# A two-layer attention encoder on one core: the global branch's output projection trails its gates by four tiles in place of three

## The chip, the cores and the metric

The kernel runs on one core of one Trainium2 chip. The metric is the device time of one execution in microseconds (us), shown as the median of several runs. One execution of it was also recorded by the hardware profiler; all rows below come from that one.

## The reference

Two layers of a hybrid block run on 528 tokens (16 learned tokens, then 512 of input), each of 1024 features in float32. Cut to what matters:

```python
def hybrid_layer(x, norm_g, w_in, q_norm_g, k_norm_g, rpb, w_o_attn, w_o_na, w_out, cos, sin):
    proj = jnp.einsum('bld,de->ble', rms_norm(x, norm_g), w_in)
    qa, ka, va, za, qb, kb, vb, zb, ga, gb = split_cols(proj)
    ...                                   # per-head norm and rotary positions for qa, ka
    oa = gqa_attention(qa, ka, va) * jax.nn.silu(za)          # the global branch
    ob = neighbourhood_attention(qb, kb, vb, rpb) * jax.nn.silu(zb)
    ya = jnp.einsum('ble,ed->bld', oa, w_o_attn)
    yb = jnp.einsum('ble,ed->bld', ob, w_o_na)
    mixed = jax.nn.sigmoid(ga) * ya + jax.nn.sigmoid(gb) * yb
    return x + jnp.einsum('bld,de->ble', mixed, w_out)
```

Global attention is 8 query heads over 2 key heads, neighbourhood attention 8 heads over a window of the token grid. After the second layer a last norm follows, and the 16 learned tokens are dropped.

## The kernel before

Activations lie with the features on the partitions and the tokens along the row. Each weight tile of 128 output features comes in two halves (the input features' upper and lower four blocks). `weights` (L232) loads a half (`raw`, SyncE's queue), casts it to the upper part `whi` on ScalarE (L240) and subtracts on GpSimd to get the lower part `wlo` (L241), three halves ahead of use; the list `order` (L207 to L222) sets in what sequence. The activations are split likewise (`hh`, `hl`), and `product` (L315) makes one output tile: for each of 8 blocks of input features three matmuls, hh with whi (L325), hl with whi (L326), hh with wlo (L327). In layer 0 a tile has 528 columns, in two stretches of 264; layer 1 drops the learned tokens in its gates and keeps 512 columns in one.

After each stretch of a product, or in its middle and at its end in layer 1, `tick` is called. It advances two objects of class `Side` (L284), which hold the attention: `side_gqa` with the 16 units of global attention per layer, `side_na` with the 8 neighbourhood heads. A unit starts when its counter, modulo 4, has a set value and its inputs are there; its parts are then due so many ticks later. So the attention's matmuls lie between those of the products. A global unit makes scores (`S`), softmax, a transposition by way of DRAM, the split `pth` and `ptl` (ScalarE L193, VectorE L194), split ends `ga` (ScalarE L896, GpSimd L898), the sum `av` (L905), its upper half copied to `cmb` (ScalarE L769) and added to `oa` (L773). The fourth block of `oa` is complete after the last unit, 7_1; it is multiplied by its gate `za` (L777) and split into `oa_3a` (ScalarE) and `oa_3b` (VectorE). A neighbourhood head has scores `Sb` (read by VectorE, L990), transposed parts (`tal`, `tbl`, `na`), sums `avb` and the result `ob`. `S` and `Sb` share one PSUM tile.

The layer ends in the merge (L1144 to L1180). First the neighbourhood branch: eight gate tiles (`merge_gate`, products 34 to 41 into `mg`), and from the fourth gate on after each one the projection tile `y` of three before (`merge_half`, L1136, weights 46 to 49). Then the global branch, with gates 26 to 33 and weights 42 to 45: gate m, then y of m less 3 from the four blocks of `oa`, the add of the other branch into `ma` (L1170) and the split `mx`. `side_na.finish()` and `side_gqa.finish()`, run before the first y tile of the branch, work off what attention is left. In layer 0 an output projection (`pp` from `mx`) follows; in layer 1 the last gate's end releases `last_split`, which splits the final weights (`wl`) on ScalarE and GpSimd, and the final matmuls `pf` (L1234 to L1236) come after the last y tile.

Of the kernel before, what the change touches and what calls it, by code (L numbers as in the profile page):

```python
# [46 lines left out]
QA, KA, VA, ZA, QB, KB, VB, ZB, GA, GB = 0, 4, 5, 6, 10, 14, 18, 22, 26, 34  # L47
WOA, WOB, WOUT = 42, 46, 50
NCHUNK = 58

LAG = 3

# [41 lines left out]
def trunk_kernel(ctx: ExitStack, tc: tile.TileContext, xT, w, gn, gf, bias, rope, out):  # L96
    nc = tc.nc
# [15 lines left out]
    def slot(tag, name, dt=F32):  # L113
        n = NKEY if tag in ("KB", "KR", "K", "E") else NTOK
        t = slots.tile([P, n], dt, tag=tag, bufs=BUFS[tag], name=name)
        return t[:, :NTOK] if tag == "E" else t
# [90 lines left out]
    order = []  # L207
    for l in range(DEPTH):
        cols = [QA, QA + 1, QA + 2, QA + 3, KA, VA]
        for j in range(4):  # L210
            cols += [KB + j, QB + j, VB + j, ZB + j, ZA + j]
        order += [(l, c, i) for c in cols for i in range(2)]
        if l == 0:

            order = order[6:]
        for gate, wo in ((GB, WOB), (GA, WOA)):
            for m in range(8 + LAG):
                order += [(l, gate + m, 0), (l, gate + m, 1)] if m < 8 else []
                order += [(l, wo + (m - LAG) // 2, (m - LAG) % 2)] if m >= LAG else []
        order += [(l, WOUT + m, i) for m in range(8) for i in range(2)] if l < DEPTH - 1 else []  # L220
    place = {key: i for i, key in enumerate(order)}
    ready, loaded = [], []  # L222
# [8 lines left out]
    def weights(l, c, half, ahead=3):  # L231
        n = place[l, c, half] + ahead  # L232
        for l_, c_, i in order[len(loaded):n + 3]:
            raw = slots.tile([P, 4 * P], F32, tag="raw", bufs=BUFS["raw"], name=f"raw{l_}_{c_}_{i}")
            nc.sync.dma_start(raw, w[l_, c_][:, 4 * P * i:4 * P * (i + 1)])
            loaded.append(raw)
        for l_, c_, i in order[len(ready):n]:
            name, raw = f"{l_}_{c_}_{i}", loaded[len(ready)]
            hi, lo = (slots.tile([P, 4 * P], F32R, tag=tag, bufs=BUFS[tag], name=tag + name) for tag in ("whi", "wlo"))
            cast = nc.scalar.copy(hi, raw)  # L240
            sub = nc.gpsimd.tensor_sub(lo, raw, hi.bitcast(F32))  # L241
            split_at["weights"] = cast.ins, sub.ins
            ready.append((hi, lo))
        return ready[place[l, c, half]]
# [22 lines left out]
    def last_split(us):  # L267
        for u in us:
            hi, lo = (((key_half if tag == "KB" else lambda name, dt: slot(tag, name, dt))(f"wl{u}{tag}", F32R))[:, :4 * P]
                      for tag in ("h", KEEP[u]))  # L270
            cast = nc.scalar.copy(hi, last_raw[u])
            sub = nc.gpsimd.tensor_sub(lo, last_raw[u], hi.bitcast(F32))
            split_at["weights"] = cast.ins, sub.ins
            last_w[u] = hi, lo

    l = 0
# [39 lines left out]
    def product(l, c, rhs, full, halves=(0, 1), name="pp", spans=None):  # L316

        ws = [weights(l, c, i) for i in halves]
        n = 4 * len(ws)
        for a, b in spans or (((0, HALF), (HALF, NTOK)) if full else ((0, NREAL),)):  # L320
            ps = bank(ps_p, f"{name}{l}_{c}_{a}", "pp")[:, :b - a]
            for i in range(n):
                wh, wl = (t[:, P * (i % 4):P * (i % 4 + 1)] for t in ws[i // 4])
                rh, rl = rhs[i]
                nc.tensor.matmul(ps, wh, rh[:, a:b], start=i == 0, stop=False)  # L325
                nc.tensor.matmul(ps, wh, rl[:, a:b], start=False, stop=False)  # L326
                nc.tensor.matmul(ps, wl, rh[:, a:b], start=False, stop=i == n - 1)  # L327
                if not full and i == 3 and n == 8:
                    tick()
            with tc.high_priority():  # L330
                yield ps, a, b
            tick()
# [121 lines left out]
    for l in range(DEPTH):  # L454
        last = l == DEPTH - 1
# [371 lines left out]
        zgate, oa, o_t, newest, sums_a = {}, [None] * 4, {}, {}, {}  # L827
# [300 lines left out]
        def merge_gate(c, m):  # L1128
            t = slot("E", f"mg{l}_{c}_{m}")
            for ps, a, b in project(c + m):  # L1130
                nc.vector.tensor_mul(t[:, a:b], ps, rbc[:, a:b])  # L1131
                split_at["gate"] = nc.scalar.activation(t[:, a:b], t[:, a:b], AF.Tanh, scale=0.5)  # L1132
            return t

        def merge_half(m, t, c, br, out, spans=None):
            for ps, a, b in product(l, c + m // 2, br, full, (m % 2,), f"y{m % 2}", spans):  # L1136
                nc.vector.scalar_tensor_tensor(out[:, a:b], t[:, a:b], 1.0, ps, op0=ALU.add, op1=ALU.mult)  # L1137
                yield a, b

        mb, gates = [], {}  # L1140
        for m in range(8 + LAG):
            if m < 8:
                gates[m] = merge_gate(GB, m)
            if m == LAG - 1:  # L1144
                side_na.finish()
                while ending:
                    ending.pop(0)()
            if m >= LAG:
                mb.append(slot("B", f"mb{l}_{m - LAG}"))
                for _ in merge_half(m - LAG, gates[m - LAG], WOB, ob, mb[m - LAG]):  # L1150
                    pass
        mixed = []
        for m in range(8 + LAG):
            if m < 8:
                gates[m] = merge_gate(GA, m)
            if last and m == 7:

                weights(l, WOA + 3, 1, 1)
                with tc.issue_after(split_at["gate"].ins):
                    last_split((0, 1, 2))  # L1160
            if m == LAG - 1:
                side_gqa.finish()
            if m >= LAG:
                ma = slot("G", f"ma{l}_{m - LAG}")
                hi, lo = two("M", f"mx{l}_{m}", F32R)
                end = m == 7 + LAG
                for a, b in merge_half(m - LAG, gates[m - LAG], WOA, oa, ma):
                    if (end and full) or b == N:
                        a = a if end else 0
                        nc.vector.tensor_add(ma[:, a:b], ma[:, a:b], mb[m - LAG][:, a:b])  # L1170
                        with ExitStack() as held:
                            if last and m in (7, 8):
                                held.enter_context(tc.issue_after(split_at["weights"][0]))
                            split(hi[:, a:b], lo[:, a:b], ma[:, a:b])
                mixed.append((hi, lo))
                if last and m in (7, 8):
                    with tc.issue_after(split_at["hi"].ins):
                        last_split(((3, 4, 5), (6, 7))[m - 7])
            if last and m == 4:
                last_load(range(KT))  # L1180

# [40 lines left out]
    for f in range(2):  # L1222
        for t in range(4):
            x = xs[f, t]
            end = f == 1 and t == 3
# [89 lines left out]
```

## Time and profile before

| | us |
|---|---|
| runs | 846.31, 846.28, 844.58; median 846.28 |
| profiled execution | 845.68, of which the span from first to last instruction is 844.0 and 1.68 lie around it |
| granted TensorE clock, mean | 0.996 of full |
| TensorE (PE) busy | 821.0, 97% of the span |
| VectorE (DVE), ScalarE (ACT), GpSimd (POOL) busy | 522.8, 474.8, 422.8 |

Matmuls are pipelined: a matmul's own duration is longer than the distance to the next one's start, and it is this distance that counts for the time. "Idle before <- releaser" says how long an engine stood still before an instruction, and what ended that.

### The profile page before, as it was taken

The numbers are of one execution on the slowest core, as the hardware profiler recorded it, in microseconds if no ns is written. First come the engines' busy times: TensorE is split into PE (matmuls) and PEld (weight loads), VectorE is DVE, ScalarE is ACT, GpSimd is POOL, SyncE is SP. The second block draws the span as 40 slices with busy tenths as digits, with TensorE's granted clock in tenths as the row PEclk, the third lists the DMA queues.
The fourth block names the chain that finished last, engine by engine and source line by source line (L and its number), as shares of the span: only waits on it lengthen the run. The fifth ranks groups of instructions, "written<-read, shape, count | busy, mean of one in ns | idle before, by whom it ended". The sixth has DMA issues, their size and how long they took to land.

```text
span 844.0 us, 16154 instructions
## 1 busy us (share of the span) xinstructions
PE 821.0 (97%) x5662; PEld 757.9 (90%) x5662; DVE 522.8 (62%) x1152; ACT 474.8 (56%) x1137; POOL 422.8 (50%) x362
## 2 busy tenths in 40 slices
PE   9999999999999999899999999999999999999997
PEld 9999999999999999899998989898988787778786
DVE  7976667676765562436547656766776556545633
ACT  8654766667864563333445456675768545543422
POOL 1664545444444453654764644444545436464851
PEclk9999999999999999999999999999999999999999
DMA  7277564667454664335555585647566566444502
GB/s 277 89 195 223 133 196 116 197 195 197 147 161 118 188 178 128 108 93 150 151 141 121 152 212 154 196 160 225 153 187 197 167 193 187 140 147 140 185 3 101
DMA packets 113249, 135.00 MB, mean 160 GB/s; under 512 B 31888, under 2 KB 66192, under 8 KB 113168
## 3 DMA queue, kind: packets, MB, share of 16 engines
q1 hardware_dynamic: 112448, 132.90, 54.0%
q8 instruction: 45, 0.74, 0.4%
q10 hardware_dynamic: 720, 1.06, 0.3%
q14 instruction: 36, 0.29, 0.1%
HBM read 98.50 MB, written 21.84 MB: 143 GB/s over the span
## 4 chain that ended last, share of the span: by engine, by line
PE 85%; DVE 6%; ACT 3%; issue 2%; DMA 2%; SPq 1%; POOL 0%; POOLq 0%; DVEq 0%; ACTq 0%
PE pp L327 18%; PE pp L325 18%; PE pp L326 18%; PE av L905 4%; PE y L326 3%; PE y L327 3%; PE y L325 3%; DVE ptl L194 2%; PE avb L1052 2%; PE S L556 2%; PE S L557 2%; PE pf L1234 2%; PE pf L1236 2%; PE pf L1235 2%; PE tb L129 1%
## 5 line engine op out<-in xcount | busy, mean ns | idle before, releaser
L241 POOL TENSOR_TENSOR wlo<-raw,whi 128x512 fp32r<-128x512 f32 x210 | 287.5, 1376 | 322.2 <-ACT whi L240 262.1
L327 PE MATMUL pp<-hh,wlo 128*128 128x264 f32 (+3 forms) x1040 | 325.8, 313 | 0.6 <-POOL wlo L241 0.6
L325 PE MATMUL pp<-hh,whi 128*128 128x264 f32 (+3 forms) x1040 | 326.1, 314 | 0.3 <-DVE ma L1137 0.3
L326 PE MATMUL pp<-hl,whi 128*128 128x264 f32 (+3 forms) x1040 | 324.0, 312 | 0.0
L327 PEld LDWEIGHTS pp<-hh,wlo 128*128 128x128 f32 x1040 | 196.4, 189 | 11.2 <-POOL wlo L241 0.8
L326 PEld LDWEIGHTS pp<-hl,whi 128*128 128x128 f32 x1040 | 196.8, 189 | 9.5
L325 PEld LDWEIGHTS pp<-hh,whi 128*128 128x128 f32 x1040 | 196.2, 189 | 9.5 <-DVE ma L1137 0.5
L240 ACT CAST whi<-raw 128x512 fp32r<-128x512 f32 x210 | 128.7, 618 | 116.5 <-PE pp L326 41.4
L867 DVE STREAM_TRANSPOSE P<-P 128x512 f32<-128x512 f32 x64 | 46.4, 726 | 38.9 <-ACT P L841 38.6
L898 POOL TENSOR_TENSOR ga<-pm,ga 32x128 fp32r<-32x128 f32 x64 | 40.4, 632 | 47.9 <-issue 26.8
L194 DVE TENSOR_TENSOR ptl<-P,pth 128x512 fp32r<-128x512 f32 x64 | 55.6, 881 | 12.8 <-ACT pth L193 10.3
L1131 DVE TENSOR_TENSOR mg<-pp,rbc 128x264 f32<-128x264 f32 (+1 forms) x48 | 24.7, 515 | 50.2 <-PE pp L327 49.5
L837 DVE CUSTOM_DVE_ANT_1 P<-S,r 128x528 f32<-128x528 f32 x64 | 44.8, 700 | 14.5 <-PE S L557 13.7
L841 ACT ACTIVATE P<-P,st 128x528 f32<-128x528 f32 x64 | 47.1, 737 | 1.7
L1132 ACT ACTIVATE mg<-mg 128x264 f32<-128x264 f32 (+1 forms) x48 | 23.7, 493 | 36.9 <-DVE mg L1131 36.8
L193 ACT CAST pth<-P 128x512 fp32r<-128x512 f32 x64 | 39.2, 612 | 1.4 <-DMA P<-turn 1.3
L905 PE MATMUL av<-ptl,VA 128*128 128x256 f32 x128 | 35.0, 299 | 4.1 <-DVE ptl L194 3.7
L992 ACT ACTIVATE bias<-bias,stb 128x208 f32<-128x208 f32 (+1 forms) x64 | 31.0, 486 | 13.3 <-DVE stb L990 13.2
L326 PE MATMUL pp<-mx,whi 128*128 128x264 f32 x128 | 36.6, 286 | 0.0
L327 PE MATMUL pp<-mx,wlo 128*128 128x264 f32 x128 | 36.4, 284 | 0.0
L325 PE MATMUL pp<-mx,whi 128*128 128x264 f32 x128 | 36.3, 284 | 0.0
L840 ACT ACTIVATE st<-st 128x1 f32<-128x1 f32 x64 | 13.0, 202 | 40.9 <-DVE st L837 40.5
(534 smaller groups left out, 1727.4 us busy)
## 6 DMA issues: line engine op xcount, KB each, us to landing
raw<-in_w_dram SPq DMA_DIRECT2D x210, 256.0 KB
turn<-P SPq DMA_DIRECT2D x32, 528.0 KB
P<-turn SPq DMA_DIRECT2D x128, 128.0 KB
bias<-in_bias_dram SPq DMA_DIRECT2D x16, 480.0 KB
KB<-KB SPq DMA_DIRECT2D x24, 272.0 KB
rawl<-in_w_dram SPq DMA_DIRECT2D x16, 256.0 KB
x<-in_xT_dram SPq DMA_DIRECT2D x8, 264.0 KB
xr<-in_xT_dram SPq DMA_DIRECT2D x8, 264.0 KB
```

The source lines that it names most:

```text
L193: split_at["hi"] = nc.scalar.copy(hi, src)
L194: split_at["any"] = nc.vector.tensor_sub(lo, src, hi.bitcast(F32))
L240: cast = nc.scalar.copy(hi, raw)
L241: sub = nc.gpsimd.tensor_sub(lo, raw, hi.bitcast(F32))
L325: nc.tensor.matmul(ps, wh, rh[:, a:b], start=i == 0, stop=False)
L326: nc.tensor.matmul(ps, wh, rl[:, a:b], start=False, stop=False)
L327: nc.tensor.matmul(ps, wl, rh[:, a:b], start=False, stop=i == n - 1)
L837: newest["max"] = nc.vector.tensor_tensor_reduce(p[:n].rearrange("p (i k) -> p i k", i=2), S[:n, :, :HALF], scale[:n].unsqueeze(2).to_broa ...
L841: nc.scalar.activation(p[:n], p[:n], AF.Exp, bias=st[:n, 1:2], scale=1.0, accum_out=st[:n, 2:3] if total is None else total)
L867: nc.vector.transpose(c["both"][:n, a:b], c["both"][:n, a:b])
L898: nc.gpsimd.tensor_sub(tm[64 + 32 * t:96 + 32 * t, n * t:n * (t + 1)], m, tm[:32, :n].bitcast(F32))
L905: nc.tensor.matmul(c["av"], rows2(c["t"][i][0]), c["t"][i][1], start=i == 0, stop=i == 8)
```

## The change

A second constant, LAG_A = 4, takes the place of LAG in the global branch of both layers: y of tile m less 4 follows gate m; the list of weight halves has the same order; `side_gqa.finish()` runs one gate later. Neighbourhood branch and arithmetic are unchanged. Line numbers after it are larger by 2.

```diff
+LAG_A = 4
...
-        for gate, wo in ((GB, WOB), (GA, WOA)):
-            for m in range(8 + LAG):
+        for gate, wo, lag in ((GB, WOB, LAG), (GA, WOA, LAG_A)):
+            for m in range(8 + lag):
                 order += [(l, gate + m, 0), (l, gate + m, 1)] if m < 8 else []
-                order += [(l, wo + (m - LAG) // 2, (m - LAG) % 2)] if m >= LAG else []
+                order += [(l, wo + (m - lag) // 2, (m - lag) % 2)] if m >= lag else []
...
-        for m in range(8 + LAG):
+        for m in range(8 + LAG_A):
             if m < 8:
                 gates[m] = merge_gate(GA, m)
-            if last and m == 7:
+            if last and m == LAG_A + 4:
                 weights(l, WOA + 3, 1, 1)
                 with tc.issue_after(split_at["gate"].ins):
                     last_split((0, 1, 2))
-            if m == LAG - 1:
+            if m == LAG_A - 1:
                 side_gqa.finish()
-            if m >= LAG:
+            if m >= LAG_A:
...
```

All other lines of the diff put `m - LAG_A` where `m - LAG` stood.

**TensorE, layer 0, where the last global unit's sum `av_7_1` meets the merge.** The first y tile is `y_42` and pp_30 is the gate after gate 29. Before:

```order
L905 MATMUL av_7_1_5081<-ga_120,VA_775 128x256
L325 MATMUL y_42_0_5175<-oa_3a,whi_42_0_5103 128x264
L325 MATMUL y_42_264_5189<-oa_3a,whi_42_0_5103 128x264
L326 MATMUL y_42_0_5175<-oa_3b,whi_42_0_5103 128x264
L327 MATMUL y_42_0_5175<-oa_3a,wlo_42_0_5104 128x264
L326 MATMUL y_42_264_5189<-oa_3b,whi_42_0_5103 128x264
L327 MATMUL y_42_264_5189<-oa_3a,wlo_42_0_5104 128x264
L325 MATMUL pp_30_0_5219<-hh_0_143,whi_30_0_5109 128x264
```

And after:

```order
L907 MATMUL av_7_1_5121<-ga_120,VA_775 128x256
L327 MATMUL pp_30_0_5180<-hh_4_190,whi_30_1_5090 128x264
L328 MATMUL pp_30_0_5180<-hl_4_191,whi_30_1_5090 128x264
L327 MATMUL pp_30_264_5207<-hh_4_190,whi_30_1_5090 128x264
L328 MATMUL pp_30_264_5207<-hl_4_191,whi_30_1_5090 128x264
L329 MATMUL pp_30_0_5180<-hh_4_190,wlo_30_1_5091 128x264
L327 MATMUL pp_30_0_5180<-hh_5_203,whi_30_1_5090 128x264
```

Behind `av_7_1` there stood the six matmuls on `oa_3a` and `oa_3b`; now the second half of pp_30 stands there, 24 matmuls that use whi_30_1 and wlo_30_1, and y_42 comes behind them. Ahead of `av_7_1`, 24 matmuls of pp_30's first half took the place of 18 of y_42; its first `av` matmul now has 19 of them ahead and five behind it.

**ScalarE, same place: the casts around the copy `cmb` of `av_7_1`.** Before:

```order
L193 CAST pth_7_1_2_5045<-P_7_1_4801 128x8x2x32
L896 CAST ga_120<-pm_7_1_4969 32x128
L769 COPY cmb_5092<-av_7_1_5081 64x256
L240 CAST whi_30_0_5109<-raw_30_0_5002 128x512
L240 CAST whi_30_1_5171<-raw_30_1_5008 128x512
L193 CAST oa_3a<-oa_3_3913 128x528
```

And after:

```order
L195 CAST pth_7_1_2_5045<-P_7_1_4801 128x8x2x32
L898 CAST ga_120<-pm_7_1_4969 32x128
L771 COPY cmb_5132<-av_7_1_5121 64x256
L242 CAST whi_30_1_5090<-raw_30_1_5002 128x512
L242 CAST whi_42_0_5170<-raw_42_0_5008 128x512
L195 CAST oa_3a<-oa_3_3913 128x528
```

The cast of whi_30_0 has moved up, to where that of whi_42_0 was; whi_30_1, which the matmuls right behind `av_7_1` now use, is cast behind the copy `cmb` that reads `av_7_1`. On GpSimd wlo_30_1 likewise stands behind the unit's `ga` and the gate product `za`.

**TensorE, layer 1, scores of a neighbourhood head (`Sb`) and of a global unit (`S`).** Before, behind the last `Sb` matmul of head 0:

```order
L557 MATMUL Sb_0_7128<-KB_00_6907,QB_0a 128x208
L325 MATMUL pp_6_0_7115<-hh_4_6121,whi_6_1_7037 128x512
L326 MATMUL pp_6_0_7115<-hl_4_6122,whi_6_1_7037 128x512
...
L325 MATMUL pp_6_0_7115<-hh_7_6342,whi_6_1_7037 128x512
L326 MATMUL pp_6_0_7115<-hl_7_6343,whi_6_1_7037 128x512
L327 MATMUL pp_6_0_7115<-hh_7_6342,wlo_6_1_7038 128x512
L728 MATMUL vtb_0_7166<-ident,vb_0_6950 128x128 x3
```

And after:

```order
L559 MATMUL Sb_0_7147<-KB_00_6907,QB_0a 128x208
L327 MATMUL pp_6_0_7134<-hh_4_6121,whi_6_1_7061 128x512
L328 MATMUL pp_6_0_7134<-hl_4_6122,whi_6_1_7061 128x512
...
L327 MATMUL pp_6_0_7134<-hh_6_6269,whi_6_1_7061 128x512
L328 MATMUL pp_6_0_7134<-hl_6_6270,whi_6_1_7061 128x512
L558 MATMUL S_0_1_1_7178<-KA1h_6925,Q_0_6533 128x264
L559 MATMUL S_0_1_1_7178<-KA1l_6926,Q_0_6533 128x264
```

Eight product matmuls now lie between the end of `Sb` and a global score that uses the same PSUM tile. All 16 units of layer 1 start three ticks (one and a half products) earlier, since `finish()` in layer 0 leaves the counter of `side_gqa` one lower; the neighbourhood heads stay where they were.

## Rows read from the trace of the kernel before

**Rows 1.** The page: the chain of work that ended last, share of the span by engine.

```profile
PE 85%; DVE 6%; ACT 3%; issue 2%; DMA 2%; SPq 1%; POOL 0%; POOLq 0%; DVEq 0%; ACTq 0%
```

**Rows 2.** The view of waits of TensorE (PE), whole span: what it waited for: us in total, times, longest us.

```profile
PE av L905 <- DVE ptl L194: 3.7, 7, 0.8
PE y L325 <- ACT oa_3a L193: 2.4, 1, 2.4
PE y L325 <- ACT ob L193: 1.5, 1, 1.5
PE y L326 <- DVE oa_3b L194: 1.1, 2, 0.6
PE avb L1052 <- DVE na L798: 0.9, 1, 0.9
```

**Rows 3.** TensorE's order in time around `av_7_1` in layer 0: start us, us, engine, line, operation, count [idle before <- releaser]. 46 matmuls start from the first row up to the last, the last row not counted.

```profile
334.89 0.28 PE L325 MATMUL y<-oa_0a,whi 128*128 128x264 f32 x1
...
337.08 0.28 PE L905 MATMUL av<-pth,VA 128*128 128x256 f32 x1
...
338.59 0.28 PE L905 MATMUL av<-ga,VA 128*128 128x256 f32 x1
341.26 0.51 PE L325 MATMUL y<-oa_3a,whi 128*128 128x264 f32 x2 [2.39 <-ACT oa_3a L193]
342.29 0.39 PE L326 MATMUL y<-oa_3b,whi 128*128 128x264 f32 x1 [0.52 <-DVE oa_3b L194]
...
343.32 0.59 PE L325 MATMUL pp<-hh,whi 128*128 128x264 f32 x1 [0.28 <-DVE ma L1137]
...
346.34 0.29 PE L326 MATMUL pp<-hl,whi 128*128 128x264 f32 x1
```

**Rows 4.** Windows of the span: stretch, its us, busy us (and instructions) of PE, weight loads, DVE, ACT, POOL, then the granted clock, DMA share and GB/s.

```profile
342.00:344.00 2.00, 1.43 (x7) 1.22 (x8) 1.37 (x4) 0.62 (x1) 2.00 (x2) 0.73 0.44 131
344.00:346.00 2.00, 2.00 (x11) 2.00 (x11) 1.30 (x2) 0.63 (x1) 2.00 (x2) 0.50 0.56 157
360.00:380.00 20.00, 20.00 (x166) 20.00 (x165) 7.40 (x14) 7.07 (x14) 9.91 (x8) 1.00 0.32 92
660.00:680.00 20.00, 18.50 (x93) 15.42 (x92) 11.85 (x21) 10.51 (x25) 9.67 (x9) 1.00 0.64 206
```

**Rows 5.** ScalarE, VectorE and GpSimd in order of time, same place as rows 3.

```profile
338.90 0.36 ACT L769 COPY cmb<-av 64x256 f32<-64x256 f32 x1 [1.38 <-PE av L905]
339.29 1.14 ACT L240 CAST whi<-raw 128x512 fp32r<-128x512 f32 x2
...
336.52 1.55 DVE L194 TENSOR_TENSOR ptl<-P,pth 128x512 fp32r<-128x512 f32 x2 [1.00 <-ACT pth L193]
...
339.99 6.33 POOL L241 TENSOR_TENSOR wlo<-raw,whi 128x512 fp32r<-128x512 f32 x4 [0.25 <-ACT whi L240]
```

**Rows 6.** ScalarE, GpSimd and VectorE in order of time in layer 1, where the last neighbourhood head meets its merge.

```profile
666.49 0.37 ACT L769 COPY cmb<-av 64x256 f32<-64x256 f32 x1 [3.77 <-PE av L905]
667.28 0.62 ACT L193 CAST ob<-ob 128x512 fp32r<-128x512 f32 x1
...
662.01 1.67 POOL L898 TENSOR_TENSOR ga<-pm,ga 32x128 fp32r<-32x128 f32 x2 [1.63 <-issue]
...
665.08 0.69 DVE L777 TENSOR_TENSOR ob<-ob,zb 128x512 f32<-128x512 f32 x1 [1.72 <-POOL zb L822]
```

**Rows 7.** TensorE in order of time in layer 1, where the last global unit meets the merge.

```profile
754.53 0.40 PE L327 MATMUL pp<-hh,wlo 128*128 128x512 f32 x1
...
755.81 0.50 PE L326 MATMUL y<-oa_3b,whi 128*128 128x512 f32 x1 [0.55 <-DVE oa_3b L194]
...
756.53 0.50 PE L325 MATMUL y<-oa_0a,whi 128*128 128x512 f32 x1
```

**Rows 8.** TensorE, then VectorE, in order of time: scores of one neighbourhood head in layer 1 and their reading. Eight `Sb` matmuls begin with the first row.

```profile
501.74 0.26 PE L556 MATMUL Sb<-KB,QB_0a 128*128 128x208 f32 x1
...
502.56 0.27 PE L557 MATMUL Sb<-KB,QB_0a 128*128 128x208 f32 x1
...
502.87 0.37 DVE L990 CUSTOM_DVE_ANT_0 bias<-Sb,bias 128x208 f32<-128x208 f32 x1 [0.99 <-PE Sb L557]
...
504.19 0.08 DVE L990 DVE_READ_ACCUMULATOR2_ANT stb<- 128x1 f32 x1
```

**Rows 9.** VectorE, then TensorE, in order of time: the keys of layer 1's global attention, and the place on TensorE behind which its first scores now stand.

```profile
485.49 1.79 DVE L547 TENSOR_TENSOR KA1l<-k,KA1h 64x544 fp32r<-64x544 f32 x2 [0.71 <-ACT KA1h L546]
...
486.49 0.27 PE L728 MATMUL vtam<-ident,va 128*64 128x128 f32 x1
```

**Rows 10.** The end of layer 1: TensorE (12 matmuls of one y tile from the first row to the second), then VectorE in order of time; the last row is VectorE in layer 0.

```profile
784.13 0.40 PE L327 MATMUL y<-oa_3a,wlo 128*128 128x512 f32 x1
...
786.90 0.40 PE L327 MATMUL y<-oa_3a,wlo 128*128 128x512 f32 x1
...
791.86 0.68 DVE L1137 SCALAR_TENSOR_TENSOR ma<-mg,y 128x512 f32<-128x512 f32 x1
792.57 1.07 DVE L1170 TENSOR_TENSOR ma<-ma,mb 128x512 f32<-128x512 f32 x1
...
795.27 0.67 DVE L1137 SCALAR_TENSOR_TENSOR ma<-mg,y 128x512 f32<-128x512 f32 x1
...
380.62 0.71 DVE L1170 TENSOR_TENSOR ma<-ma,mb 128x528 f32<-128x528 f32 x1
```

More of the change, by code (lines that the diff above doesn't have):

```diff
@@ L1160, in trunk_kernel @@
                     last_split((0, 1, 2))
-            if m == LAG - 1:
+            if m == LAG_A - 1:
                 side_gqa.finish()
-            if m >= LAG:
-                ma = slot("G", f"ma{l}_{m - LAG}")
+            if m >= LAG_A:
+                ma = slot("G", f"ma{l}_{m - LAG_A}")
                 hi, lo = two("M", f"mx{l}_{m}", F32R)
-                end = m == 7 + LAG
-                for a, b in merge_half(m - LAG, gates[m - LAG], WOA, oa, ma):
+                end = m == 7 + LAG_A
+                for a, b in merge_half(m - LAG_A, gates[m - LAG_A], WOA, oa, ma):
                     if (end and full) or b == N:
                         a = a if end else 0
-                        nc.vector.tensor_add(ma[:, a:b], ma[:, a:b], mb[m - LAG][:, a:b])
+                        nc.vector.tensor_add(ma[:, a:b], ma[:, a:b], mb[m - LAG_A][:, a:b])
                         with ExitStack() as held:
-                            if last and m in (7, 8):
+                            if last and m - LAG_A in (4, 5):
                                 held.enter_context(tc.issue_after(split_at["weights"][0]))
@@ L1175, in trunk_kernel @@
                 mixed.append((hi, lo))
-                if last and m in (7, 8):
+                if last and m - LAG_A in (4, 5):
                     with tc.issue_after(split_at["hi"].ins):
-                        last_split(((3, 4, 5), (6, 7))[m - 7])
+                        last_split(((3, 4, 5), (6, 7))[m - LAG_A - 4])
             if last and m == 4:
```

## The prediction

> **What bounds the kernel now.** I read first the page's chain, then TensorE's waits, then the order in time around the largest of them. The chain lies on TensorE for 85% [rows 1], and the engine is busy for 97% of the span, so only two things can pay: TensorE's idle times, and stretches where its clock is low. The view of waits names few [rows 2]: 2.4 us before the first matmul on oa_3a, 1.1 us in two waits on oa_3b, 1.5 us on the last block ob of the neighbourhood branch, and 4.6 us in small waits inside the attention (ptl, na). The change touches the first four.
>
> The order in time shows what the one in layer 0 costs. From the first y matmul at 334.89 to 346.34, 46 matmuls start [rows 3]. At the undisturbed pace of 20 us for 166 matmuls, 0.1205 us each [rows 4], they need 5.54 us; they took 11.45. So **5.9 us are lost there**, more than the waits say: 4.5 us in the waits and the slow starts around them, and 1.45 us in the clock. After the waits the granted clock stood at 0.50, the 1.2 GHz level, for all of 344 to 346 [rows 4], and the 13 matmuls from 343.32 to 346.34 took 3.02 us for 1.57 [rows 3].
>
> **The change, part by part.**
>
> *The join in layer 0, −3.5 us.* Behind `av_7_1` the order puts pp_30's second half in place of the matmuls on oa_3. With 19 matmuls ahead in place of 18, av begins at about 337.18 in place of 337.08; its fifth pair still waits for ptl, which ends at 338.07 [rows 5], and its last matmul starts about 0.16 later than before, at 338.75. The copy `cmb` came 0.31 after the last av, and the next cast 0.39 after `cmb` [rows 3, 5]: that cast is now whi_30_1, from 339.45 to 340.05 (half of the 1.14 that two took, and the write). TensorE has nothing else ahead of it in its queue: a **new wait** of 1.2 us, from 338.87 to 340.05. Four matmuls follow (0.5). The fifth needs wlo_30_1. GpSimd began 0.70 after the cast's start [rows 5], now 340.15, and took 1.58 for one of four, so 341.73: a second wait of 1.2. Then 20 matmuls (2.4 us) run to 344.1, and under them oa_3a is cast (about 340.7 to 341.4) and oa_3b subtracted; y_42 finds both ready. The loss of 5.9 becomes 2.4. Ends: no new wait, −5.9; and the clock falls as before, −2.05. I take −3.5, since both new waits are worked out from the rows of the very instructions.
>
> *The same join in layer 1, −1.1 us.* There four distances between matmuls took 2.00 us, from 754.53 to 756.53 [rows 7]; at 0.231 each (12 in 2.77, [rows 10]) they need 0.92. With a whole gate product behind av_7_1, 24 times 0.231 or 5.5 us, both casts are done, and whi_30_1 stands where no copy holds it up for long. Ends: −1.1 and 0.
>
> *The neighbourhood join in layer 1, −1.5 us.* TensorE waits 1.5 us for ob [rows 2]. ob was late since zb stood on GpSimd behind the 1.67 us of ga of unit 4_1, VectorE waited 1.72 for zb, and the cast of ob stood behind `cmb` of the same unit, which waited 3.77 for av_4_1 [rows 6]. By the order unit 4_1 is now past that point when the last head ends: its ga comes before the head's sums, av_4_1 has one matmul left, and 12 product, 4 score and 9 y matmuls (about 5.4 us) lie ahead of the first use of ob. Ends: −1.5 and 0.
>
> *The shared score tile, +1.0 us.* As the global units of layer 1 start three ticks earlier, the second score of a unit comes in the same tick as a head's `Sb`, with eight matmuls (or 14 of the short form) between, and may not write before VectorE has read `Sb`. In the trace of before, reading ends at 504.27, 1.71 after the start of the last `Sb` matmul [rows 8]; eight matmuls later is 502.67 + 8 x 0.231 = 504.52. So 0.2 us to spare, if VectorE is free. It is busy 62% of the time; with what is left of one operation of 0.70 spread evenly, a head waits 0.62 x (0.5 x 0.5 / 2 / 0.7) = 0.11 us, eight heads 0.9. No wait on this tile is in the rows of before, so the bounds are wide: −2.3, if half of the 4.6 us of small waits [rows 2] go in the new phase, and +5, if each head meets a split pair like the 1.55 of ptl [rows 5] at its middle, 0.78 less 0.2. I stay near the row in which VectorE was ready.
>
> *First scores of layer 1, +0.3 us.* They now stand right behind vtam, 486.49, and need KA1l, which VectorE finishes at 487.28 [rows 9]; one score and two product matmuls lie between. Ends: 0 and +0.5.
>
> *The end, +0.6 us.* Behind the last gate come five y tiles in place of four. A tile takes TensorE 2.77 us, but VectorE, ScalarE and VectorE again (ma, add, mx) take 3.41 from tile to tile [rows 10]. One tile more in that chain ends the last mx later by 0.64 against TensorE, which already has almost no slack there. The final matmuls can't hide it, their last ones being the ones that use it. Ends: 0 and +1.0. One row speaks for the lower end: the add took 1.07 beside GpSimd's splits of the final weights and 0.71 alone [rows 10], and those splits, released by the last gate, begin one tile earlier as seen from the end. The Trainium skill (SBUF — State Buffer, section Who interferes with whom) states that a VectorE instruction with two SBUF inputs contends with a GpSimd instruction that reads SBUF; the trace agrees, 1.07 against 0.71. By that rule, with the splits out of the way, the tile would take 3.05 and the term be +0.3; I keep 0.6, since the splits still last through most of the tiles.
>
> *Loads, at nothing.* The sequence of weight loads has the same length, and the moved halves stay three ahead of use; no matmul waited for a load in the view of waits. If that cover went, it would show as a cast waiting for its raw.
>
> **The sum:** −3.5 − 1.1 − 1.5 + 1.0 + 0.3 + 0.6 = −4.2, against the profiled execution's 845.68: **841.5 us**. That execution lies 0.6 below the median of the runs, 846.28. About 0.2%, 1.7 us, can be told from no change.
>
> **The rivals.**
>
> *The clock falls all the same.* Two waits of 1.2 us with four matmuls between may be as bad as one of 2.4 with a few behind it. For it: in the trace of before the clock fell after 2.39, 0.52 and 0.28 us of idleness with six matmuls among them [rows 3, 4], 3.2 us in all against 2.4 now. Against it: the single wait of 1.5 us for ob left the clock at 1.00 [rows 2, 4]. It gives back 1.45: 843.0. The Trainium skill (TensorE: Matmul & The Clock Gate, section A second HAM failure mode: psum-queue depth-cycling) states that frequent short idle times between groups of matmuls, and not only one long one, can make the clock swing between its levels. By that rule this rival is the forecast; no row of before shows short waits alone doing it.
>
> *The wait only changes its name.* whi_30_1 and wlo_30_1 come later than worked out (GpSimd still at za, the cast behind something I took for done), TensorE stands as long as before in layer 0, and the layer 1 joins lose what the score tile costs. Then −1.1 − 1.5 + 1.0 + 0.3 + 0.6 = −0.7: 845.0. For it: the same chain av, cmb, cast stands there. Against it: it is shorter by the add, the gate product and oa_3b.
>
> *Slower: the score tile becomes the bound of layer 1.* Each of its eight heads would hold the global score that follows; VectorE's queue has softmax, transposition and split pairs of the neighbouring unit in just that tick. With w us per head the sum is −5.2 + 8w; it passes +1.7 from w = 0.86, and with a whole split pair ahead, w = 1.35, it gives +5.6: 851.3. For it: only 0.2 us to spare [rows 8]. Against it: VectorE began to read 0.31 us after the last `Sb` matmul in the row of before, and it idles a third of the time.
>
> **How the numbers follow.** Forecast 0.57; clock rival 0.20; name rival 0.14; slower rival 0.09. The forecast's own range, with half the bounds of its terms, is 839 to 844; it and the clock rival lie below 844.0, but for the upper edge. The range reaches to the name rival: **838.8 to 845.0**; what is left out is the slower rival and the far ends of the terms. Faster by over 0.2%: 0.74 (0.77 of the first two less their upper edges); within 0.2%: 0.17; slower: 0.09.
>
> **What would show it.** In the profile after: no wait of TensorE on oa_3a or oa_3b, and none on ob; two waits near 339 to 342, on whi (ScalarE) and wlo (GpSimd), of about 1.2 us each; granted clock at 1.00 in that stretch; waits on VectorE's reading of `Sb` before global scores in layer 1, about 1 us in all; one of some 0.3 on KA1l; and some 1 us of waits on mx among the final matmuls, 0.6 more than now. The prediction is wrong if the clock falls to 0.50 behind those two waits, if the wait on whi is over 2 us, or if layer 1 shows waits of the score tile of over 4 us.

## The result, and the profile after

The changed kernel took **841.01 us** (median of 5 runs, 837.82 to 842.12) against 845.47 (5 runs, 844.58 to 846.31): ratio **0.9942**, interval 0.9919 to 0.9965. The profiled execution took 842.12, of which 840.4 is the span, 3.6 less than the span of before. It was the slowest of its five, so the two traces show less than the medians do.

The view of waits of TensorE in the kernel after (columns as in [rows 2]):

```profile
PE av L907 <- DVE ptl L196: 2.4, 4, 1.0
PE S L558 <- DVE stb L992: 2.3, 2, 1.9
PE pp L329 <- POOL wlo L243: 2.1, 3, 1.0
PE pp L327 <- ACT whi L242: 1.1, 1, 1.1
PE S L559 <- DVE KA1l L549: 0.2, 1, 0.2
```

The waits on oa_3a, oa_3b, ob and na are gone. In their place stand waits on whi and wlo, and on VectorE's reading of the score tile (stb). No wait on mx is in the view. TensorE where `av_7_1` meets the merge in layer 0, the counterpart of [rows 3]:

```profile
338.19 0.28 PE L907 MATMUL av<-ga,VA 128*128 128x256 f32 x1
339.56 0.39 PE L327 MATMUL pp<-hh,whi 128*128 128x264 f32 x1 [1.09 <-ACT whi L242]
...
341.33 0.59 PE L329 MATMUL pp<-hh,wlo 128*128 128x264 f32 x1 [1.01 <-POOL wlo L243]
341.71 0.42 PE L327 MATMUL pp<-hh,whi 128*128 128x264 f32 x1
...
344.57 0.38 PE L327 MATMUL pp<-hh,whi 128*128 128x264 f32 x1
```

The first two waits are those forecast: 1.09 on whi_30_1 behind the last `av` matmul, four matmuls, 1.01 on wlo_30_1. But behind the second wait the distance between two starts is 0.22 in place of 0.12, until 344.57. The windows say why, the counterpart of [rows 4]:

```profile
340.00:342.00 2.00, 0.99 (x6) 0.77 (x5) 1.14 (x2) 1.70 (x4) 2.00 (x2) 0.84 0.01 4
342.00:344.00 2.00, 2.00 (x11) 2.00 (x11) 0.07 (x1) 0.00 (x0) 2.00 (x2) 0.50 0.46 132
```

The granted clock stood at 0.50, the 1.2 GHz level, from 342 to 344, so in this execution the clock fell behind the two short waits, as it had before behind the longer ones on oa_3a and oa_3b. ScalarE, then GpSimd, at the same place [rows 5]:

```profile
338.50 0.36 ACT L771 COPY cmb<-av 64x256 f32<-64x256 f32 x1 [1.55 <-PE av L907]
338.89 1.14 ACT L242 CAST whi<-raw 128x512 fp32r<-128x512 f32 x2
...
337.90 1.28 POOL L824 TENSOR_TENSOR za<-za,sumsa 128x512 f32<-128x512 f32 x1
339.59 5.88 POOL L243 TENSOR_TENSOR wlo<-raw,whi 128x512 fp32r<-128x512 f32 x4 [0.41 <-ACT whi L242]
```

The casts of whi_30_1 and whi_42_0 start 0.39 after `cmb`, and GpSimd, free since 339.18, begins wlo_30_1 0.70 after the cast's start, both as worked out.

Where the last neighbourhood head meets the merge of layer 1 (GpSimd, ScalarE, TensorE; [rows 6]), zb no longer stands behind ga, and TensorE takes the last block of ob without a wait, 2.08 after its first y matmul at 665.49:

```profile
663.34 1.30 POOL L824 TENSOR_TENSOR zb<-zb,sumsb 128x512 f32<-128x512 f32 x1
...
665.54 0.62 ACT L195 CAST ob<-ob 128x512 fp32r<-128x512 f32 x1
...
665.49 0.40 PE L327 MATMUL y<-ob,whi 128*128 128x512 f32 x1
...
667.57 0.40 PE L327 MATMUL y<-ob,whi 128*128 128x512 f32 x1
```

The longest new wait of layer 1 is on the shared score tile. SyncE's queue, then VectorE, then TensorE:

```profile
641.65 0.33 SPq L872 DMA_DIRECT2D turn<-P  x1
...
643.37 0.44 SPq L976 DMA_DIRECT2D bias<-in_bias_dram  x1
...
651.64 0.37 DVE L992 CUSTOM_DVE_ANT_0 bias<-Sb,bias 128x208 f32<-128x208 f32 x1 [2.52 <-DMA bias<-in_bias_dram]
...
653.09 0.39 PE L558 MATMUL S<-KA1h,Q 128*128 128x264 f32 x1 [1.91 <-DVE stb L992]
```

VectorE was free for 2.52 us before it read `Sb` of head 7; it waited for that head's bias, 480 KB, which SyncE issued at 643.37, behind a transfer (`turn` of unit 4_1, which carries the unit's scores to DRAM) that its queue did not issue before 641.65. The second score of unit 5_0 waited 1.91 us for the tile. In the trace of before the same load stood ahead of that `turn`, which came at 648.85:

```profile
641.02 0.41 SPq L974 DMA_DIRECT2D bias<-in_bias_dram  x1
```

The other wait on the score tile is of another kind. VectorE, then TensorE:

```profile
566.20 0.36 DVE L992 CUSTOM_DVE_ANT_0 bias<-Sb,bias 128x208 f32<-128x208 f32 x1
...
567.65 0.39 PE L558 MATMUL S<-KA1h,Q 128*128 128x264 f32 x1 [0.41 <-DVE stb L992]
```

Here VectorE came to `Sb` straight from other work, with no idle time ahead, 0.96 us after the start of the last `Sb` matmul (565.24).

The end, VectorE then TensorE [rows 10]:

```profile
781.91 0.67 DVE L1139 SCALAR_TENSOR_TENSOR ma<-mg,y 128x512 f32<-128x512 f32 x1
...
784.38 0.69 DVE L196 TENSOR_TENSOR mx<-ma,mx 128x512 fp32r<-128x512 f32 x1 [0.69 <-ACT mx L195]
784.99 0.68 DVE L1139 SCALAR_TENSOR_TENSOR ma<-mg,y 128x512 f32<-128x512 f32 x1
...
788.42 0.68 DVE L1139 SCALAR_TENSOR_TENSOR ma<-mg,y 128x512 f32<-128x512 f32 x1
...
788.67 0.39 PE L329 MATMUL y<-oa_3a,wlo 128*128 128x512 f32 x1
789.15 0.50 PE L1236 MATMUL pf<-wl0h,mx 128*128 128x512 f32 x1
```

VectorE takes 3.08 and 3.43 from tile to tile, and the first final matmul starts 0.48 after the last y matmul where 0.23 is the pace. In the experiment with the larger lag in layer 1 alone the trace names the releaser of that matmul: VectorE's ma, not mx.

Cut into stretches by the starts of four TensorE instructions (the scores' transposition tb near 241, the first output projection matmul of layer 0, vtam in layer 1, the first pf matmul; last column: to the start of the last matmul), the traces compare as follows, in us. In the line of before, tb starts at 241.18, the projection at 388.76, vtam at 486.49, pf at 792.68, the last matmul at 837.72; the other lines are read in the same way. "Again" is the changed kernel's second profile; the rest are the experiments below. "New phase" is the earlier start of layer 1's global units, which the change brings along with the lag.

| kernel | tb to projection (layer 0's join) | to vtam | vtam to pf (layer 1) | pf to last |
|---|---|---|---|---|
| before | 147.58 | 97.73 | 306.19 | 45.04 |
| after | 145.85 | 97.73 | 304.96 | 45.18 |
| after, again | 145.89 | 97.79 | 303.04 | 45.18 |
| larger lag in layer 0 alone | 144.18 | 97.80 | 306.11 | 45.00 |
| larger lag in layer 1 alone | 148.56 | 97.73 | 305.94 | 45.13 |
| new phase alone | 148.81 | 97.79 | 302.77 | 45.06 |
| whi_30_1 early | 143.50 | 97.73 | 305.34 | 45.16 |
| whi_30_1 early, lags 4 and 3 | 143.30 | 97.73 | 301.71 | 45.07 |

The untouched stretch in the middle agrees within 0.07 in all of them. That is not so everywhere: ahead of tb, where no instruction was moved either, the start of tb lies between 239.66 and 241.18 in the thirteen profiles of this document, and the old join of layer 0 took 147.58, 148.56 and 148.81. So a difference between two profiles counts here only where a wait or the clock in the rows accounts for it. Ahead of tb after stands 0.57 earlier than before: that part of the 3.6 is not the change's.

### The profile page after: what moved, and what is told of

Its sections match the earlier page's. It is cut to its first block, busy times and chain, and to the rows that moved or that the text cites. A ratio compares the mean times of both kernels' runs of the same rounds, so it can differ in the third digit from the quotient of the medians.

```text
span 840.4 us, 16156 instructions
## 1 busy us (share of the span) xinstructions
PE 821.2 (98%) x5662; PEld 758.9 (90%) x5662; DVE 521.4 (62%) x1152; ACT 474.4 (56%) x1137; POOL 424.4 (50%) x362
## 4 chain that ended last, share of the span: by engine, by line
PE 79%; DVE 7%; DMA 5%; ACT 4%; issue 2%; SPq 1%; POOL 1%; POOLq 0%; DVEq 0%; ACTq 0%
PE pp L329 17%; PE pp L328 17%; PE pp L327 17%; PE av L907 4%; PE y L329 3%; PE y L328 3%; PE y L327 3%; PE S L558 2%; PE S L559 2%; PE avb L1054 2%; PE pf L1236 2%; PE pf L1238 2%; PE pf L1237 2%; DMA bias<-in_bias_dram 1%; DVE ptl L196 1%
## 5 line engine op out<-in xcount | busy, mean ns | idle before, releaser
L900 POOL TENSOR_TENSOR ga<-pm,ga 32x128 fp32r<-32x128 f32 x64 | 42.2, 660 | 61.6 <-issue 32.6
L907 PE MATMUL av<-pth,VA 128*128 128x256 f32 x128 | 34.6, 291 | 0.0
```

The lines of the kernel that those rows point to most:

```text
L900: nc.gpsimd.tensor_sub(tm[64 + 32 * t:96 + 32 * t, n * t:n * (t + 1)], m, tm[:32, :n].bitcast(F32))
L907: nc.tensor.matmul(c["av"], rows2(c["t"][i][0]), c["t"][i][1], start=i == 0, stop=i == 8)
```

## The experiments

**The larger lag in layer 0 alone.** LAGS is a lag for each layer; the added tick restores the phase that layer 1 had.

```diff
-LAG_A = 4
+LAGS = (4, 3)
...
             if m == LAG_A - 1:
                 side_gqa.finish()
+                if not last:
+                    side_gqa.now += 1
```

> The larger lag in layer 0 alone: layer 1 keeps a lag of three, and the counter of the global units is set so that layer 1 has the phase of before. Theory (the parts add up, each worth what the two traces show at its place): the three waits on oa_3a, oa_3b and ma give way to two on whi_30_1 and wlo_30_1 of about 1.1 and 1.0 us, the clock still falls to 0.50 behind them, -1.7 us, so 843.8 against 845.5; layer 1 shows the waits of before (ob 1.5, oa_3b 0.55, no wait on the score tile). Rival (the clock fell by chance in the one execution that was profiled): the clock stays at 1.00 behind the two waits, -3.5 or so, 842.

Measured 841.25 (840.80 to 843.32), ratio 0.9962 (0.9949 to 0.9974): −3.2 us. TensorE, and windows:

```profile
338.73 0.39 PE L327 MATMUL pp<-hh,whi 128*128 128x264 f32 x1 [1.10 <-ACT whi L242]
...
340.48 0.39 PE L329 MATMUL pp<-hh,wlo 128*128 128x264 f32 x1 [1.00 <-POOL wlo L243]
...
340.00:342.00 2.00, 1.52 (x12) 1.52 (x13) 0.99 (x1) 1.01 (x2) 2.00 (x2) 1.00 0.24 71
342.00:344.00 2.00, 2.00 (x18) 2.00 (x18) 0.86 (x2) 1.27 (x3) 2.00 (x3) 1.00 0.52 184
```

The two waits are there, 1.10 and 1.00, and the clock stayed at 1.00: the rival's case. The join costs 144.18 in place of 147.58, −3.4, the forecast's −3.5. Layer 1 shows the waits of before. The profiled execution was the shortest of the five: it and two others (841.22, 841.25) show a mean granted clock of 0.999, the two longer ones (842.56, 843.32) 0.997. So the clock may well have fallen in two of the five; where, no row of theirs shows.

**The larger lag in layer 1 alone**: LAGS = (3, 4), without the added tick.

> The larger lag in layer 1 alone, layer 0 and the phase of layer 1 as before. Theory: only the wait on oa_3b in layer 1 goes (-1.1 with the slow start around it), and the end gains at most 0.6 us in waits on mx: between -1.1 and -0.5, 844.4 to 845.0; ob still waits 1.5. Rival (the join in layer 1 was hidden, since the layer's end is bound by VectorE's chain of 3.4 us a tile): no change, 845.5, with the 1.1 us back as waits on mx among the last matmuls.

Measured 844.34, ratio 0.9995 (0.9986 to 1.0004): no change. TensorE in the join of layer 1, and at the end:

```profile
755.66 0.50 PE L327 MATMUL y<-oa_3a,whi 128*128 128x512 f32 x1 [0.21 <-ACT oa_3a L195]
...
792.10 0.50 PE L1236 MATMUL pf<-wl0h,mx 128*128 128x512 f32 x1 [0.16 <-DVE ma L1139]
```

In the old phase the wait on oa_3 stays, 0.21, with slow starts around it: the stretch vtam to pf gains 0.25, and the end loses 0.09. So neither theory nor rival quite: the lag alone doesn't clear that join. The order says why: between the last `av` matmul and the first on oa_3a stand 11 matmuls before, 15 here, 20 with the new phase alone, and 44 with both.

**The new phase alone**: a lag of three in both layers.

```diff
             if m == LAG - 1:
                 side_gqa.finish()
+                if not last:
+                    side_gqa.now -= 1
```

> The earlier start of layer 1's global units alone: a lag of three in both layers, the counter of the global units one lower when layer 1 begins. Theory: the wait on ob (1.5) and one on na (0.9) go, waits of the shared score tile come (2.3 us in two), one on KA1l (0.2) and one on wlo (0.6): within 1 us of before, 844.5 to 846. The larger wait on the score tile stands where VectorE waits for head 7's bias, whose load is queued on SyncE behind the transfer turn of unit 4_1. Rival (the new phase is what carries the gain, and the wait for the bias in the profiled execution was an accident): -2.5 or more, 843 or less, and no wait of the score tile over 0.5 us in this profile.

Measured 842.34 (841.51 to 843.12), ratio 0.9968 (0.9957 to 0.9980): −2.7 us. Layer 1 gains 3.42 (306.19 to 302.77): the theory of "within 1 us" fell, the rival holds. VectorE at head 7, and TensorE's only wait on the score tile:

```profile
652.57 0.38 DVE L990 CUSTOM_DVE_ANT_0 bias<-Sb,bias 128x208 f32<-128x208 f32 x1 [0.45 <-DMA bias<-in_bias_dram]
...
570.51 0.39 PE L556 MATMUL S<-KA1h,Q 128*128 128x264 f32 x1 [0.42 <-DVE stb L990]
```

VectorE waited 0.45 for the bias here, and TensorE did not wait for that head's tile. The join with oa_3 in layer 1 shows no wait either, with a lag of three.

**The changed kernel once more.**

> The changed kernel itself once more, for the spread between its executions (837.8 to 842.1 so far). Theory: the same waits at the same places as in its first profile, with the clock falling behind whi_30_1 and wlo_30_1 and a wait of 1.9 us for head 7's bias, about 841. Rival (waits that hang on when a transfer lands come and go): the wait for the bias, or the fall of the clock, is missing in this profile, and the time is 838 to 839 in such an execution.

Measured 839.05 (837.12 to 839.86), ratio 0.9925 (0.9913 to 0.9938). Its profile, windows and VectorE at head 7:

```profile
342.00:344.00 2.00, 2.00 (x11) 2.00 (x11) 0.43 (x1) 0.29 (x1) 2.00 (x3) 0.50 0.51 181
...
649.04 0.38 DVE L992 CUSTOM_DVE_ANT_0 bias<-Sb,bias 128x208 f32<-128x208 f32 x1 [0.37 <-DMA bias<-in_bias_dram]
```

The clock fell again, and the wait of 1.91 us is missing: issue to reading took 6.1 us (642.92 to 649.04) where it had taken 8.3 (643.37 to 651.64). The rival holds in one half: the wait for the bias comes and goes, and layer 1 differs by 1.92 between the two profiles (304.96 and 303.04).

**whi_30_1 ahead of `cmb`** in the changed kernel:

```diff
+            if not last and m == LAG_A - 1:
+                weights(l, GA + LAG_A, 1, 1)
+                split_at["early"] = split_at["weights"]
             if m < 8:
                 gates[m] = merge_gate(GA, m)
...
+            with ExitStack() as held:
+                if full and "early" in split_at:
+                    held.enter_context(tc.issue_after(split_at["early"][0]))
+                nc.scalar.copy(t[r, :n], av[q, :n])
```

> The changed kernel, with whi_30_1 of layer 0 cast ahead of the copy cmb of av_7_1 on ScalarE; nothing else in the order differs. Theory (the two waits are ScalarE's and GpSimd's queues): the wait on whi_30_1 goes, and the one on wlo_30_1, still behind ga and za on GpSimd, starts earlier and grows from 1.0 to about 1.7 us (za's end to wlo's end, 1.3, and what is left of za). The loss falls from 2.1 to 1.7 us: 0.4 faster than the changed kernel, 838.6 to 840.6, less if the clock stays at 1.00 behind one wait. Rival (whi comes late for its raw data, not for its place in the queue): the wait stays on whi at about 1.1 us.

Measured 837.09 (836.06 to 839.74), ratio 0.9909 (0.9896 to 0.9922). TensorE, and windows:

```profile
340.00 0.39 PE L329 MATMUL pp<-hh,wlo 128*128 128x264 f32 x1 [1.51 <-POOL wlo L243]
...
650.44 0.39 PE L558 MATMUL S<-KA1h,Q 128*128 128x264 f32 x1 [1.89 <-DVE stb L995]
...
340.00:342.00 2.00, 2.00 (x16) 2.00 (x17) 0.99 (x3) 1.17 (x3) 2.00 (x2) 1.00 0.38 128
652.00:654.00 2.00, 2.00 (x10) 1.90 (x10) 1.68 (x4) 1.64 (x4) 0.00 (x0) 0.50 0.01 2
```

One wait of 1.51 on wlo_30_1 is left (forecast 1.7), the clock stays at 1.00 behind it, and the join takes 143.50, 2.4 less than after. The wait for the bias, 1.89, was in this profile, and here the clock fell to 0.50 behind that single wait, which it had not in after (1.00 from 652 to 656, behind 1.91). This execution took 839.74, the four others 836.06 to 837.17.

**wlo_30_1 ahead of the gate product za as well**: the product of the last unit comes one tick later, and with `issue_after` behind the early subtraction.

> The same, and on GpSimd wlo_30_1 ahead of the gate product za. Theory: one wait of about 0.4 us on wlo_30_1 is left (ga's end plus 1.3, against the end of the four matmuls on whi_30_1), the loss falls by 1.7 us, and with so little idle time the clock stays at 1.00, which gives back up to 1.5 us more in executions in which it fell: 836 to 838.5. Rival (za, now later, holds up the last block of oa): a wait on oa_3a of over 0.5 us among the matmuls of y_42, and no gain over the changed kernel.

Measured 838.47 (836.36 to 839.18), ratio 0.9918: not faster than whi_30_1 alone. TensorE, then VectorE:

```profile
338.90 0.39 PE L329 MATMUL pp<-hh,wlo 128*128 128x264 f32 x1 [0.29 <-POOL wlo L243]
...
342.51 0.36 PE L327 MATMUL y<-oa_0a,whi 128*128 128x264 f32 x1 [0.88 <-DVE mg L1143]
...
340.13 1.77 DVE L782 TENSOR_TENSOR oa<-oa,za 128x528 f32<-128x528 f32 x1 [1.15 <-POOL za L830]
341.94 0.43 DVE L1143 TENSOR_TENSOR mg<-pp,rbc 128x264 f32<-128x264 f32 x1
```

The wait on wlo_30_1 is down to 0.29, but za is late: VectorE's product with it starts at 340.13 and takes 1.77 us, the gate's instruction mg queued behind it frees its PSUM bank late, and TensorE waits 0.88 there. The join takes 143.37, 0.13 less. The rival holds in substance, with mg in place of oa_3a.

**Each head's bias in layer 1 one tick earlier**: a step of head hd at tick 3 loads the bias of hd + 1.

> The changed kernel, with the bias of each neighbourhood head of layer 1 loaded one tick earlier, so that head 7's load stands ahead of unit 4_1's transfer turn on SyncE. Theory (the long wait on the score tile is that load, queued behind a transfer that waits for VectorE): no wait of VectorE on bias, none of TensorE on the score tile over 0.5 us, in any execution; the slow executions (842) go, the fast ones stay: 837.5 to 839.5. Rival (the score tile is held by VectorE's other work): the wait on the score tile stays, with VectorE busy ahead of its reading.

Measured 842.16 (839.99 to 843.27), ratio 0.9963 (0.9949 to 0.9976): slower than the changed kernel's second measurement (0.9925), and not to be told from its first (0.9942). The bias is there in time, but other waits of TensorE came, on pth (0.72 where after had 0.20 on ptl) and whi:

```profile
541.34 0.39 PE L908 MATMUL av<-pth,VA 128*128 128x256 f32 x1 [0.72 <-ACT pth L196]
...
633.60 0.51 PE L328 MATMUL pp<-hh,whi 128*128 128x512 f32 x1 [0.54 <-ACT whi L243]
```

Of SyncE's queue, the transfers back of unit 4_0 (P from turn) began at 635.36, behind a weight load issued at 634.94, where they had begun at 626.74 in the second profile of after. The theory is right on the wait and wrong on the time; that the moved loads cause the new waits is likely by this row, and not shown wait by wait.

**All of these, with lags of 4 and 3.**

> The three together, and a lag of three in layer 1 (the new phase of the global units stays): four in layer 0, whi_30_1 and wlo_30_1 early, bias early. Theory: the parts add. Against the changed kernel -1.7 at the join of layer 0, up to -1.5 of the clock, the wait for the bias, and -0.3 for the shorter chain of y tiles at the end, as the join on oa_3 in layer 1 shows no wait in the new phase with either lag: 835 to 837.5. Rival (with a lag of three the join in layer 1 waits again): a wait on oa_3b there of 0.5 us, and no gain over the kernel with whi and wlo early.

Measured 839.06 (838.77 to 839.73), ratio 0.9929. It has the waits that the two kernels before it brought, 0.91 on mg, and 0.59 on pth and 0.55 on whi in layer 1. The time of the theory was missed by 1.6 us, since it had taken those two parts for gains.

**whi_30_1 early, lags 4 and 3**: the kernel with whi_30_1 early, and LAGS = (4, 3).

> whi_30_1 of layer 0 early as in the kernel with that alone, a lag of four in layer 0 and of three in layer 1, new phase kept. Theory (the larger lag is worth nothing in layer 1, since the new phase alone takes away its wait on oa_3, and costs a tile in the end's chain): 0.2 to 0.4 faster than with four in both, 836.7 against 837.1. Rival (the lag in layer 1 keeps the join from waiting): a wait on oa_3 in layer 1 and 0.5 to 1.1 slower.

Measured **836.19** (835.23 to 836.52), ratio **0.9890** (0.9875 to 0.9905), the fastest here. No wait on oa_3 in layer 1. The profile is free of the wait for the bias (issued 641.07, read 647.06) and of the fall of the clock behind it, which together make most of the difference between 305.34 and 301.71. Neither profile with whi_30_1 alone early has the wait of 0.96 on ptl that after has at 716, so the gain over after is not the join's alone.

**whi_30_1 early, and only head 7's bias one tick earlier**: `hd == 6` is the condition of the added step.

> whi_30_1 early, four in both layers, and only head 7's bias one tick earlier, so that SyncE issues it ahead of unit 4_1's turn; the other heads' loads stay. Theory: the wait of 1.9 us on the score tile before unit 5_0's second score, which hangs on that load, is absent in every execution, and none of the waits on pth and whi that came when all heads' loads were moved: 835.5 to 837, with a smaller spread than 836.1 to 839.7. Rival (the load is late because the DMA engines are busy, not for its place in the queue): the wait stays, 837 to 839.

Measured 837.55 (837.14 to 838.09), ratio 0.9907. The wait is absent in the profile, and the four executions lie within 1 us (837.14 to 838.09), but there is no gain: the median is not below that of whi_30_1 alone (837.09). Missed by half a microsecond. Two waits stand in this profile that whi_30_1 alone, with lags of 4 and 4 or of 4 and 3, does not have: 0.96 on ptl at 712 and 0.32 on tal at 654.

**The same with lags 4 and 3.**

> Both: whi_30_1 early, four in layer 0 and three in layer 1, head 7's bias early. Theory: the parts add, 835.2 to 836.7, the fastest of all. Rival (a lag of three in layer 1 with the load earlier makes a new wait): not below the better of the two others.

Measured 836.91 (836.65 to 836.98), ratio 0.9900: 0.6 below the same with four in layer 1 (vtam to pf 302.95 against 303.78, and 0.08 at the end), and 0.7 above the one that leaves the bias where it was; the intervals of those two (0.9885 to 0.9915 and 0.9875 to 0.9905) overlap. So it is not the fastest of all, and the parts did not add. In the profiles its layer 1 takes 1.24 more than that other one's, 302.95 against 301.71, and the same two waits make up most of it, 0.96 on ptl and 0.31 on tal. VectorE, GpSimd and TensorE here, then VectorE and GpSimd in the one that leaves the bias:

```profile
709.48 1.79 DVE L197 TENSOR_TENSOR ptl<-P,pth 128x512 fp32r<-128x512 f32 x1
...
709.43 1.29 POOL L244 TENSOR_TENSOR wlo<-raw,whi 128x512 fp32r<-128x512 f32 x1
...
711.32 0.39 PE L911 MATMUL av<-ptl,VA 128*128 128x256 f32 x1 [0.96 <-DVE ptl L197]
...
710.07 0.69 DVE L196 TENSOR_TENSOR ptl<-P,pth 128x512 fp32r<-128x512 f32 x1
...
710.23 1.68 POOL L243 TENSOR_TENSOR wlo<-raw,whi 128x512 fp32r<-128x512 f32 x1
```

The two subtractions overlap, and whichever starts first runs at its own length. Where GpSimd is 0.05 ahead, VectorE's takes 1.79 and TensorE waits for it; where VectorE is 0.16 ahead, its takes 0.69 and TensorE doesn't wait.

## Why the prediction was right, point by point

The time, 841.0 against 841.5, is nearer than the reasons deserve, and part of that is luck: the same kernel measured again gave 839.05, in the profiled execution the largest gain came at half its size, and in layer 1 terms that were not forecast cancelled one that was put too low.

*The join in layer 0 (−3.5).* The mechanism and both waits came as worked out: 1.09 and 1.01 for 1.2 and 1.2. (One reading was wrong without consequence: the `av` matmul of before that started late behind ptl, at 338.13, is of the third pair, not a fifth.) What failed is the condition that the clock stays, and the prediction had listed its fall behind these two waits among the signs of being wrong. In after it fell, and the join gained 1.73 (147.58 to 145.85); the clock rival had said −2.05. In the kernel with the lag in layer 0 alone it stayed, and the gain was 3.4. So the sum −3.5 was right for one case, and the rival, with 0.20, is what three of the four profiles with these two waits show (after, again, and the kernel with all heads' bias early: 0.50 in their windows from 342 to 344). The Trainium skill's rule on short idle times, which the prediction weighed there (TensorE: Matmul & The Clock Gate, section A second HAM failure mode: psum-queue depth-cycling), agrees with these three profiles and not with the fourth. Behind one wait of 1.5 us at this join the clock stayed at 1.00 in all four profiles that have it. And the loss before was itself larger in other executions: the old join took 148.56 and 148.81 in the two experiments that kept it, with the clock at 0.50 for longer. Over whole executions the lag in layer 0 alone gives 3.2 us by the ratio, 3.4 by the medians.

*The join on oa_3 in layer 1 (−1.1).* The wait went, but not by the lag: the lag alone left the stretch at −0.25, the phase alone removed it. The step that failed took the order of the changed kernel, in which both had moved, for the lag's doing: of its "whole gate product" between the last `av` matmul and oa_3a the lag alone gives 4 matmuls (15 for 11). With the phase alone it is 20, and no wait is left.

*The join on ob (−1.5).* Right; by the phase, as the prediction had it.

*The shared score tile (+1.0).* The place was right, the cause half. One wait, 0.41 in after and 0.39 again, is the one forecast: VectorE came late to `Sb`. The other, 1.91 or nothing, hangs on the load of a bias. The prediction costed the loads at nothing, since they had stood ahead of their use; it had not looked at what the moved `turn` transfers are queued ahead of on SyncE. Here that term was mis-sized: it was +0.4 or +2.3 in waits, and more in an execution in which the clock falls behind the long one, as it did with whi_30_1 early.

*KA1l (+0.3).* 0.20.

*The end (+0.6).* 0.25 at the first pf matmul and 0.14 behind it, 0.4 in all: smaller, since one tile in four found GpSimd idle in its last subtraction (mx, 0.69 against 1.02) and took 3.08. The add kept its 1.07 in that tile too, so it was not the add that got shorter. The prediction's row for that, 0.71 "alone", was misread: GpSimd's wlo started at 380.77, while that add ran (380.62 to 381.33), and took 1.72 where its shortest rows have 1.29. The two instructions ran beside each other in both rows, and in each the later one was the longer for it. And TensorE waited not for mx but for ma. All seven profiles with a lag of four in layer 1 start the first pf matmul 0.47 to 0.57 after the last y matmul, the six with three 0.23 to 0.30, and the last stretch is some 0.1 longer too: in layer 1 the lag is a small loss at the end. Lags of 4 and 3 against 4 and 4 with head 7's bias early differ by more, 0.6 us in the medians; there a wait of 0.48 on the score tile is in the one profile and not in the other.

*Not forecast:* the new phase also takes the wait on na (0.86) away and reduces those on ptl in layer 1, from 3.21 (six) to 1.83 (three), and brings one of 0.56 on wlo. With these, the phase alone is worth 3.4 us in layer 1 where the bias is in time (306.19 to 302.77). In after, where it isn't, phase and lag together take 1.23 away, near the 1.3 that the terms for oa_3, ob, score tile and KA1l forecast together: the gains not forecast paid for the long wait on the bias. The prediction had put the six small waits into a bound, −2.3, and taken +1.0.

*The slower rival* needed waits of 0.86 per head; the heads other than 7 show one of 0.41 in after. *The rival that the wait changes its name* came true in kind (whi, wlo) but not in size.

## What to carry to other kernels

A change of a lag moves everything whose start is counted in the same ticks: ask for each stretch which of the moved things removes a wait, and undo them one by one before crediting one of them. When a moved step issues a transfer that must wait for its data, look at what stands behind it on the issuing queue: here a load of 480 KB was wanted 5.75 us after its issue (643.37 to 649.12, when VectorE was free) where it had been read 7.73 after it before (641.02 to 648.75). And where two short waits follow each other on TensorE, look at the clock behind them too: removing the earlier of the two gave 2.35 us at that join (145.85 to 143.50), of which 1.67 is what the clock's fall costs there (145.85 against 144.18, the same two waits with the clock at 1.00).

## What the runs showed of the hardware

The same two waits, 1.1 and 1.0 us with four matmuls between, were followed by a granted clock of 0.50 in three profiles and of 1.00 in one. One wait of 1.5 us left it at 1.00 every time (on tal near 241 in all thirteen profiles, on wlo_30_1 in four, on ob in three), one of 1.72 and one of 1.91 did so too, and one of 1.89 was followed by 0.50. The Trainium skill (TensorE: Matmul & The Clock Gate, section What's actually happening) states that the chip's look at TensorE's activity runs free of the kernel, so that the point at which the clock changes differs from run to run; the different outcomes behind like waits agree with that, though none of these profiles shows the mechanism.

The same 480 KB load, issued behind the same `turn`, was read 6.0 to 6.2 us after its issue in three profiles (after again, the new phase alone, the fastest kernel, in which it was there before VectorE wanted it) and 8.1 to 8.3 in three others (after, whi_30_1 early, and that with wlo_30_1 early). Why, no row here tells.

Where VectorE's ptl subtraction and GpSimd's wlo subtraction meet in layer 1, near 710 to 715, 0.2 us in their starts decides over a wait of TensorE. In seven profiles of the new phase GpSimd starts 0.04 to 0.05 ahead, ptl takes 1.79 and TensorE waits 0.96 or 0.97 for it. In three (whi_30_1 early with either lag in layer 1, and that with wlo_30_1 early) VectorE starts 0.16 ahead, ptl takes 0.68 or 0.69, wlo 1.67 or 1.68, and TensorE has no such wait.
